# Down projections of a SwiGLU block by seven products of halves, with part of the sums on GpSimd

## The chip, the cores and the metric

The kernel runs on one core of one Trainium2 chip. A core has TensorE (PE, matrix products, with its weight loads shown apart as PEld), VectorE (DVE), ScalarE (ACT), GpSimd (POOL), SyncE (SP, which here only issues DMAs) and 16 DMA engines. Each engine works through its own instructions in order; semaphores order them against each other. SBUF is the working memory of 128 partitions, PSUM takes the results of PE. The metric is the device time of one execution in microseconds; the kernel before is given as the median of three runs.

## The reference

Two layers of a hybrid decoder on 512 tokens with 16 learned tokens ahead of them (528 columns here), model width 1024, all in float32. Each layer does an attention and retention part, and then the part that is changed:

```
hn = rmsnorm(h, ffn_norm_g)
ff = silu(hn @ w_gate) * (hn @ w_up)     # width 2816 = 22 blocks of 128
h  = h + ff @ w_down                     # back to 1024 = 8 blocks of 128
```

A last RMSNorm follows, and the 16 tokens are dropped.

## The kernel before

**Layout.** Activations lie transposed: features on the partitions, tokens on the columns. `h` is eight tiles of 128 x 528. Layer 0 works on all 528 columns in two halves of 264; in layer 1 the 16 learned tokens are no longer needed after attention, so its feed-forward part works on 512 columns (halves of 256). `w` is the width of a half.

**Precision.** Every product is made of three matmuls in a reduced format: each float32 operand is split into a high part (a cast on ACT) and a low part (a difference on DVE, in the attention stages often on POOL), and high x high, high x low and low x high are added in PSUM. So each weight block and each activation costs a split ahead of its use.

**The feed-forward loop** (`ffn`, from L794) goes over the 22 blocks of the inner width ("f blocks") in six rounds, `ROUNDS`: 0-2, 3-6, 7-10, 11-14, 15-18, 19-21. The gate and up projections of blocks 0 to 2 are dense (`dense_steps`, L217). From block 3 on a class `Unit` does gate and up of one f block together, by seven products instead of eight: the two weight matrices make up the rows of a 2 x 2 block matrix, the two halves of the model width its columns, and the two column halves of the activations the other matrix. Sums of weight blocks (`Sw`, tile `s`) and of activation blocks (`t_form`, made once per layer by `x_forms`) enter the products. A unit's weights are four conversions, the jobs `w1` to `w4`; its products are `head` (numbers 1 and 2), `middle` (6, 5, 7) and `tail` (4, 3), each of 12 matmuls (`product`, L872, matmul at L881). They accumulate into one bank from `psum_a` (x, a pool of 4 banks) and the two banks of one tile from `psum` (z and y, a pool of 2 tiles). Between products, `keep` has ACT copy the bank x into the tile `e` (L947); `done` adds z and y, applies the SiLU, multiplies, and splits the activation into `ah` and `al`, of which eight pairs of tiles exist (`act_tile`).

**Down projections** of a round are done during the next round, as fills between the products of its units: each unit takes one pair of output blocks (2p and 2p+1; four pairs in a round). `down_job` loads and splits the weights of the pair, and `down` multiplies densely: for each of the two outputs, each f block of the round, and three part products. In layer 0 there is one matmul per column half, in layer 1 one of all 512 columns (L1016). The result is copied by ACT into a tile `S` (L1023, L1025) and added into `h` by an accumulating DMA issued by POOL (L1026); in the last rounds DVE adds it. What is left when a round has only three units is done after them. The down projections of round 5 end the stage.

**Weights.** All raw weights come by DMAs issued on SP. A unit loads `w_gate`, `w_up` and half of `w_up` again into `Sw`; POOL issues two accumulating DMAs on top of these (L908, L909), so that some sums are made by the DMA. Three further sums are made by DVE (L917, L928 and the negated split L919).

**Order.** The list `steps` is the written order of PE's work. At the first matmul of a product, `need(j)` asks for the conversion of job j and of the two jobs behind it, loads included. Converted weights lie in two rings, chosen by the parity of the job's number, of two buffers each for the high and for the low part: four jobs in all. A conversion can begin when the job four before it has had its last matmul. Raw weights have three buffers (`raw`), two (`fraw`) and two (`Sw`). A scheduler of the framework puts the instructions of each engine into a fixed order ahead of the run; instructions under `high_priority` go ahead of others that are ready.

## Time and profile before

| | |
|---|---|
| median of three runs | 1272.64 us (1271.05 to 1273.75) |
| the profiled execution | 1271.96 us |
| its span, first to last instruction | 1270.1 us |
| clock granted to PE | 0.999 of full speed |

The span is what the engines' records cover; the profiled execution's own time is 1.9 us more, which lies around them. The feed-forward stages are about 300 to 616 us (layer 0) and 940 to 1240 us (layer 1). In the rows that follow, a group has its line in the kernel, its engine and operation, the tiles written and read, the shape, the count, the busy time in us, the mean of one in ns, and the engine's idle time before it with what ended it. A timeline row has start and duration in us.

### The profile page before, as it was taken

The page shows a single profiled execution, that of the slowest core. Times are in us where ns is not written, and L with a number is a line of the kernel's source. Part 1 is how long each engine was busy: PE and PEld are TensorE (multiplying, and loading weights), DVE is VectorE, ACT ScalarE, POOL GpSimd, SP SyncE. Part 2 cuts the span into 40 slices and gives each one's busy share as a digit, 9 for nine tenths or more (in the row PEclk, how much of TensorE's full clock was granted, in tenths as well). Part 3 has the DMA queues.
Part 4 walks back from the last instruction along what each step waited for, and adds up shares of the span by engine and source line. Part 5 has one row for each costly group of instructions (what it writes and reads, how often), then busy time and mean ns, then how long its engine had stood idle before and what let it go on. Part 6 is the DMA issues. An engine that isn't in the chain of part 4 may idle for free.

```text
span 1270.1 us, 24076 instructions
## 1 busy us (share of the span) xinstructions
PE 1255.0 (99%) x9271; PEld 1196.9 (94%) x9271; DVE 914.1 (72%) x1689; ACT 720.6 (57%) x1326; POOL 386.2 (30%) x662
## 2 busy tenths in 40 slices
PE   9999999999999999999999999999999999999997
PEld 8999999999999999999999989998789999999996
DVE  8877756779766666666786877477896666666766
ACT  7666545676555555554456665557765555555544
POOL 3355546421122222220025545554202222222100
PEclk9999999999999999999999999999999999999999
DMA  6322222225687777774323222222358887787721
GB/s 218 94 72 86 88 84 77 66 68 164 173 189 184 184 184 184 182 182 120 100 77 118 68 97 79 84 83 67 126 144 196 185 196 184 184 189 184 171 78 67
DMA packets 71315, 167.53 MB, mean 132 GB/s; under 512 B 8208, under 2 KB 15120, under 8 KB 71200
## 3 DMA queue, kind: packets, MB, share of 16 engines
q1 hardware_dynamic: 50576, 128.70, 31.7%
q0 software_dynamic: 20160, 36.97, 17.9%
q8 instruction: 73, 1.20, 0.4%
q14 instruction: 42, 0.34, 0.1%
q10 hardware_dynamic: 464, 0.32, 0.1%
HBM read 146.79 MB, written 2.13 MB: 117 GB/s over the span
## 4 chain that ended last, share of the span: by engine, by line
PE 92%; DVE 3%; DMA 2%; ACT 2%; issue 0%; DVEq 0%
PE psd L217 29%; PE psa L881 19%; PE psd L1016 14%; PE psd L881 13%; PE psa L217 5%; PE psa L1016 4%; PE psa L418 2%; PE psa L573 2%; PE psa L507 2%; PE psa L730 1%; PE psa L700 1%; DMA raw<-w_in 0%; DMA dec<-decay 0%; ACT whi L191 0%; PE psa L290 0%
## 5 line engine op out<-in xcount | busy, mean ns | idle before, releaser
L194 POOL TENSOR_TENSOR wlo<-raw,whi 128x128 fp32r<-128x128 f32 x504 | 259.1, 548 | 287.9 <-ACT whi L191 287.8
L217 PE MATMUL psd<-xh,whi 128*128 128x264 f32 (+1 forms) x792 | 195.8, 315 | 0.4 <-ACT whi L191 0.4
L217 PE MATMUL psd<-xh,wlo 128*128 128x264 f32 (+1 forms) x792 | 186.7, 303 | 0.0
L217 PE MATMUL psd<-xl,whi 128*128 128x264 f32 (+1 forms) x792 | 186.2, 302 | 0.4 <-DVE xl L320 0.4
L217 PEld LDWEIGHTS psd<-xh,whi 128*128 128x128 f32 x792 | 128.3, 189 | 5.4 <-ACT whi L191 1.1
L217 PEld LDWEIGHTS psd<-xh,wlo 128*128 128x128 f32 x792 | 127.0, 188 | 6.3 <-DVE wlo L194 0.4
L217 PEld LDWEIGHTS psd<-xl,whi 128*128 128x128 f32 x792 | 127.6, 189 | 4.7 <-DVE xl L320 0.8
L191 ACT CAST whi<-raw 128x512 fp32r<-128x512 f32 (+1 forms) x168 | 98.4, 613 | 49.6 <-PE psd L217 37.4
L908 POOL DMA_DIRECT2D Sw<-w_up x38 | 34.2, 899 | 230.5 <-DMA Sw<-w_up 146.4
L909 POOL DMA_DIRECT2D fraw<-w_gate x38 | 33.3, 875 | 210.5 <-DMA fraw<-w_up 65.9
L870 DVE TENSOR_TENSOR fwlo<-raw,fwhi 128x1024 fp32r<-128x1024 f32 (+2 forms) x62 | 64.0, 1033 | 38.1 <-ACT fwhi L869 38.0
L870 DVE TENSOR_TENSOR wlo<-raw,whi 128x1024 fp32r<-128x1024 f32 (+2 forms) x62 | 62.9, 1015 | 36.7 <-ACT whi L869 36.5
L869 ACT CAST whi<-raw 128x1024 fp32r<-128x1024 f32 (+2 forms) x62 | 54.9, 885 | 46.2 <-PE psd L881 37.0
L869 ACT CAST fwhi<-raw 128x1024 fp32r<-128x1024 f32 (+2 forms) x62 | 55.6, 897 | 42.8 <-PE psd L881 36.7
L917 DVE TENSOR_TENSOR Sw<-Sw,raw 128x512 f32<-128x512 f32 x38 | 26.3, 692 | 72.4 <-DMA raw<-w_gate 71.4
L1026 POOL DMA_DIRECT2D h<-S x64 | 59.9, 936 | 50.1 <-ACT S L1023 26.8
L881 PE MATMUL psa<-th,whi 128*128 128x264 f32 (+1 forms) x232 | 65.5, 283 | 0.0
L881 PE MATMUL psa<-th,wlo 128*128 128x264 f32 (+1 forms) x232 | 65.4, 282 | 0.0
L881 PE MATMUL psa<-tl,whi 128*128 128x264 f32 (+1 forms) x232 | 65.3, 282 | 0.0
L881 PE MATMUL psa<-th,fwhi 128*128 128x264 f32 (+1 forms) x224 | 63.5, 283 | 0.3 <-ACT e L947 0.3
L881 PE MATMUL psa<-tl,fwhi 128*128 128x264 f32 (+1 forms) x224 | 63.3, 283 | 0.0
L881 PE MATMUL psa<-th,fwlo 128*128 128x264 f32 (+1 forms) x224 | 63.2, 282 | 0.0
(344 smaller groups left out, 4027.3 us busy)
## 6 DMA issues: line engine op xcount, KB each, us to landing
raw<-w_in SPq DMA_DIRECT2D x54, 512.0 KB, 3.5
raw<-w_gate SPq DMA_DIRECT2D x44, 512.0 KB, 6.4
fraw<-w_up SPq DMA_DIRECT2D x38, 512.0 KB, 5.6
raw<-w_down SPq DMA_DIRECT2D x64, 256.0 KB, 2.9
Sw<-w_up SPq DMA_DIRECT2D x38, 256.0 KB, 2.6
fraw<-w_gate POOLq DMA_DIRECT2D x38, 256.0 KB, 4.3
Sw<-w_up POOLq DMA_DIRECT2D x38, 256.0 KB, 6.0
h<-S POOLq DMA_DIRECT2D x32, 264.0 KB, 5.5
```

The lines of the kernel that those rows point to most:

```text
L191: pin(nc.scalar.copy(hi, job["raw"][:, c0:c1]), pinned)
L194: pin(sub(lo[:, i:i + step], job["raw"][:, c0 + i:c0 + i + step], hi[:, i:i + step].bitcast(F32)), pinned)
L217: nc.tensor.matmul(ps[1][b][:, 0:c1 - c0], w[:, wk, :], x[:, c0:c1], start=(k == 0 and i == 0), stop=(k == n - 1 and i == 2))
L418: nc.tensor.transpose(ps[:, 128 * j:128 * j + 128], src[:, o:o + 128], idt)
L869: nc.scalar.copy(hi, src)
L870: nc.vector.tensor_sub(lo, src, hi.bitcast(F32))
L881: nc.tensor.matmul(bank()[:, 0:b.shape[-1]], a[:, o + k, :], b, start=(fresh and k == 0 and i == 0), stop=(k == n - 1 and i == 2), skip_gr ...
L908: nc.gpsimd.dma_start(s[:, HB:NK], w_up[l, self.f][:, 0:HB], accum_op=ALU.add)
L909: nc.gpsimd.dma_start(self.t["b"][:, 0:HB], w_gate[l, self.f][:, 0:HB], accum_op=ALU.add)
L917: nc.vector.tensor_add(s[:, 0:HB], s[:, HB:NK], a[:, 0:HB])
L1016: nc.tensor.matmul(v[:, 0:c1 - c0], a[:, s * n + k, :], b[:, c0:c1], start=(k == 0 and i == 0), stop=(k == n - 1 and i == 2))
L1026: nc.gpsimd.dma_start(two(h[m]), c, accum_op=ALU.add)
```

## The change

The down projections of the four rounds of four f blocks (1 to 4) no longer multiply densely. A new class `Down` takes the place of `down_job` and `down` for them: the two outputs of a pair are the rows of a 2 x 2 block matrix, the two halves of a round's four f blocks its columns, and the column halves of the activations the other matrix. Its seven products use 2 x 3 matmuls each. Parts of it:

- **Activations.** f blocks 3 to 18 no longer leave a tile pair `ah`, `al` each. When the second block of a pair of neighbours is done, seven forms of half width (blocks and their differences) are split and stored in `slots`, in two new tiles of seven forms and one of three, whose remaining four lie in halves of the state tiles `xh`, `xl` that are no longer read. POOL makes the first difference of a pair, DVE the other three. Rounds 0 and 5 keep their old tiles, which now lie in the first of the new ones. The f blocks of `w_down` are ordered on the host so that the halves lie together.
- **Weights of a Down.** POOL makes two sums and four differences of 128 x 128; one difference of 256 columns is DVE's. Fourteen blocks are split instead of eight, by two jobs.
- **Far units.** Units from f block 7 on have their sum at L917 made by POOL, in four instructions. For all units the sum of L928 goes into `s` instead of `a`, and is made at the second job instead of the fourth. Units and Downs marked `far` ask three jobs ahead instead of two.
- **Order.** From round 2 on, the products of a unit and of its Down alternate by lists written out by hand. Products 4 and 3 of a round's first Down go into the next unit (`hang`). The fourth Down of round 4 follows the units of round 5 by itself and its result is added by DVE.

```diff
         def act_tile(f):
-            return fft(f"ah{f % 8}"), fft(f"al{f % 8}")
+            t = buf(0).rearrange("p i s c -> p (i s c)")
+            i = f if f < PLAIN else f - ROUNDS[-1][0]
+            return [t[:, (2 * i + j) * T:(2 * i + j + 1) * T] for j in range(2)]
+
+        def slot(q, s, j):
+            i = (1, 2, 0)[q % 3]
+            if i < 2 or s < 3:
+                return buf(i)[:, j, s]
+            return st["x"][s - 3][j][:, HC[1][0]:HC[1][1]]
...
         def need(j):
-            for i in range(j, min(j + 3, len(jobs))):
+            for i in range(j, min(j + (4 if jobs[j].get("far") else 3), len(jobs))):
...
                     nc.gpsimd.dma_start(self.t["b"][:, 0:HB], w_gate[l, self.f][:, 0:HB], accum_op=ALU.add)
+                    if self.far:
+                        for i in range(HB):
+                            nc.gpsimd.tensor_add(s[:, i], s[:, HB + i], self.t["a"][:, i])
...
             def make2(self, hi, lo):
                 a, s = self.t["a"], self.t["s"]
-                nc.vector.tensor_add(s[:, 0:HB], s[:, HB:NK], a[:, 0:HB])
+                if not self.far:
+                    nc.vector.tensor_add(s[:, 0:HB], s[:, HB:NK], a[:, 0:HB])
                 nc.scalar.activation(hi, s, AF.Copy, scale=-1.0)
                 nc.vector.scalar_tensor_tensor(lo, s, -1.0, hi.bitcast(F32), ALU.mult, ALU.subtract)
+                nc.vector.tensor_add(s[:, 0:HB], a[:, HB:NK], s[:, 0:HB])
...
-                fh, fl = act_tile(self.f)
-                split(fh[:, c], fl[:, c], u[:, c])
-                acts[self.f] = (fh, fl)
...
+                q, second = divmod(self.f - PLAIN, 2)
+                if not second:
+                    us[q] = u2, two(tt("tq"))
+                    nc.gpsimd.tensor_sub(us[q][1][:, 0], u2[:, 1], u2[:, 0])
+                    return
+                u0, ta = us.pop(q)
+                tb = two(tt("tq"))
+                parts = [(0, 1, u0[:, 0:1]), (1, 2, u2), (3, 2, ta), (5, 2, tb)]
+                for i, (s, n, src) in enumerate(parts):
+                    if i == 2:
+                        nc.vector.tensor_sub(tb[:, 0], u2[:, 1], ta[:, 0])
+                        nc.vector.tensor_sub(tb[:, 1], u2[:, 1], u0[:, 1])
+                        nc.vector.tensor_sub(ta[:, 1], u2[:, 0], tb[:, 0])
+                    ph, pl = slots(q, s, n, 0), slots(q, s, n, 1)
+                    m = n // len(ph)
+                    for j in range(len(ph)):
+                        split(ph[j], pl[j], src[:, j * m:(j + 1) * m])
...
+        class Down:
...
+            def load(self):
...
+                r = self.t["r"] = wp.tile([128, NK, 128], F32, name="raw", tag="raw", bufs=3)
+                for s in range(2):
+                    nc.sync.dma_start(r[:, s * HB:s * HB + HB], w_down[l, 2 * self.m + s, :, self.f0:self.f1])
+                sd = self.t["s"] = tt(("nwt", "sqh")[self.m % 2])[:, 0:512].rearrange("p (k c) -> p k c", k=HB)
+                for k in range(2):
+                    nc.gpsimd.tensor_add(sd[:, 2 + k], r[:, 4 + k], r[:, 6 + k])
+                for k in range(2):
+                    nc.gpsimd.tensor_sub(sd[:, k], sd[:, 2 + k], r[:, k])
+                for k in range(2):
+                    nc.gpsimd.tensor_sub(r[:, 4 + k], r[:, k], r[:, 4 + k])
+
+            def make_a(self, hi, lo):
+                splits(hi[:, 0:HB], lo[:, 0:HB], self.t["r"][:, 0:HB])
+                splits(hi[:, HB:NK], lo[:, HB:NK], self.t["s"])
+
+            def make_b(self, hi, lo):
+                r = self.t["r"]
+                nc.vector.tensor_sub(r[:, 2:4], r[:, 2:4], self.t["s"][:, 0:2])
+                splits(hi, lo, r[:, 2:NK])
...
+            def keep(self, i):
+                def go():
+                    if i == 0:
+                        self.t["e"] = fft("S", F32, (128, 4, w), 2)
+                    e = self.t["e"][:, i]
+                    with tc.high_priority():
+                        nc.scalar.copy(e, self.t["x"][:, 0:w])
+                        if i == 3:
+                            nc.vector.tensor_add(e, self.t["y"][:, 0:w], e)
+                    if i == 2:
+                        self.add(1)
+                return go
...
+            def done(self):
+                e = self.t["e"][:, 0:2]
+                with tc.high_priority():
+                    nc.vector.tensor_add(e, self.t["zy"][:, :, 0:w], e)
+                self.add(0)
...
+                job, o, s, b, fresh, final, then = {
+                    1: (0, 0, 0, x, True, False, self.keep(0)), 2: (0, 2, 1, z, True, True, None),
+                    6: (0, 4, 5, x, False, False, self.keep(1)), 5: (0, 6, 3, y, True, False, None),
+                    7: (1, 2, 6, x, False, False, self.keep(3)), 4: (1, 4, 4, x, False, True, self.keep(2)),
+                    3: (1, 0, 2, y, False, True, self.done)}[i]
...
-                u = Unit(f)
+                u = Unit(f, r > 1)
+                if r > 1 and fills:
+                    p = fills.pop(0)[0]
+                    if p == 0:
...
+                        order = ((u, 1), (u, 2), (u, 6), (u, 5), (u, 7), (d, 1), (d, 2), (u, 4), (d, 6), (d, 5), (u, 3), (d, 7))
+                    else:
...
+                        order = [(u, 1)] + hang + [(u, 2), (d, 1), (u, 6), (d, 2), (u, 5), (d, 6), (u, 7), (d, 5), (d, 7),
+                                                   (u, 4), (d, 4), (d, 3), (u, 3)]
+                    hang = [(d, 4), (d, 3)] if p == 0 else []
+                    for o, i in order:
+                        steps += o.p(i)
+                    continue
...
             for p, g0, g1 in fills:
+                if r > 1:
+                    d = Down(p, r - 1, False)
+                    d.second()
+                    for i in (1, 2, 6, 5, 7, 4, 3):
+                        steps += d.p(i)
+                    continue
```

More of the change, by code (lines that the diff above doesn't have):

```diff
@@ L800, in ffn, with buf, slots @@
         sgs, acts = {}, {}
-        held = []
+        held, bufs, us = [], [], {}
         def two(t):
             return t[:, t0:T].rearrange("p (a b) -> p a b", a=2)
+        def buf(i):
+            if not bufs:
+                bufs[:] = [fft(f"ab{j}", shape=(128, 2, 7 if j < 2 else 3, w)) for j in range(3)]
+            return bufs[i]
         def act_tile(f):
-            return fft(f"ah{f % 8}"), fft(f"al{f % 8}")
+            t = buf(0).rearrange("p i s c -> p (i s c)")
[6 more added lines that the diff above has]
+            return st["x"][s - 3][j][:, HC[1][0]:HC[1][1]]
+        def slots(q, s, n, j):
+            i = (1, 2, 0)[q % 3]
+            return [buf(i)[:, j, s:s + n]] if i < 2 or s < 3 else [slot(q, s + k, j).unsqueeze(1) for k in range(n)]
         def g_done(f):
@@ L888, in ffn, with __init__ @@
         class Unit:
[L889 removed]
+            def __init__(self, f, far=False):
                 self.f = f
+                self.far = far
                 self.t = {}
[L892 removed]
+                self.w1 = add_job(load=self.load, make=self.make1, n=NK, far=far)
             def rest(self):
[L895 to L896 removed]
+                self.w2 = add_job(load=self.load, make=self.make2, n=NK, far=self.far)
+                self.w3 = add_job(load=self.load, make=self.make3, n=NK, far=self.far)
             def last(self):
[L899 removed]
+                self.w4 = add_job(load=self.load, make=self.make4, n=HB, far=self.far)
             def load(self):
@@ L1037, in ffn @@
         fills = []
+        hang = []
         for r, (f0, f1) in enumerate(ROUNDS):
@@ L1386 @@
     order = [0, 4, 1, 5, 2, 6, 3, 7]
+    forder = [f0 + i for f0, f1 in ROUNDS for i in ((0, 2, 1, 3) if f1 - f0 == 4 else range(f1 - f0))]
     wo = a["w_out"].reshape(DEPTH, 8, 128, D)[:, order].reshape(DEPTH, 2, 4, 128, 4, 2, 128).transpose(0, 1, 4, 3, 5, 2, 6).reshape(DEPTH, 2, 4, 128, 8, 128)
```

64 lines of the change are left out of this document (55 added, 9 removed).

## The prediction, made before the result was known

> **What bounds the kernel now.** I first read the page's shares of the engines, then how both feed-forward stages (about 300 to 616 us and 940 to 1240 us) look in a window of each, columns as on the page (PE, PEld, DVE, ACT, POOL busy with counts, granted clock, DMA share, GB/s).
>
> ```profile
> PE 1255.0 (99%) x9271; PEld 1196.9 (94%) x9271; DVE 914.1 (72%) x1689; ACT 720.6 (57%) x1326; POOL 386.2 (30%) x662
> 400.00:450.00 50.00, 50.00 (x414) 50.00 (x414) 33.21 (x46) 25.67 (x42) 11.26 (x13) 1.00 0.77 181
> 1000.00:1050.00 50.00, 49.69 (x342) 45.96 (x342) 34.68 (x47) 25.91 (x39) 10.48 (x12) 1.00 0.81 188
> ```
>
> PE never rests and its clock is full, so matmuls taken away shorten the run unless something else becomes late. DVE (66 to 69% here) is the nearest to that. The 99% does not say what a matmul costs; matmuls overlap, so I take the step from one start to the next in the timeline of PE.
>
> ```profile
> 429.80 0.29 PE L881 MATMUL psa<-xh,fwhi 128*128 128x264 f32 x1
> ...
> 437.10 0.29 PE L1016 MATMUL psa<-ah,whi 128*128 128x264 f32 x1
> ...
> 1000.54 0.40 PE L1016 MATMUL psd<-ah,whi 128*128 128x512 f32 x1
> ...
> 1002.39 0.39 PE L1016 MATMUL psd<-ah,wlo 128*128 128x512 f32 x1
> 1002.62 0.28 PE L881 MATMUL psa<-xh,whi 128*128 128x256 f32 x1
> ...
> 1005.35 0.28 PE L881 MATMUL psd<-xh,wlo 128*128 128x256 f32 x1
> ```
>
> Between the first two rows lie 60 matmuls of 264 columns: 7.30/60 = 0.1217 us each. Eight steps of 512 columns take 1.85 us: 0.231 each. Twenty-three steps of 256 columns take 2.73 us: 0.1187 each. Two matmuls of 256 cost only 0.006 us more than one of 512.
>
> **The products.** A dense down pair is 2 outputs x 4 f blocks x 3 products of high and low parts. Layer 0 does each on two column halves (48 matmuls of 264), layer 1 on all 512 columns at once (24). Seven products of halves are 7 x 2 x 3 = 42 matmuls in both layers, of 264 or 256 columns. Rounds 1 to 4 have 16 pairs per layer.
> Layer 0: 16 x 6 x 0.1217 = 11.7 us saved. Layer 1: 16 x (24 x 0.231 - 42 x 0.1187) = 16 x (5.54 - 4.99) = 8.9 us. Together 20.6 us of PE.
> A unit with its pair falls from 132 x 0.1217 = 16.06 to 126 x 0.1217 = 15.33 us in layer 0, and from 84 x 0.1187 + 24 x 0.231 = 15.51 to 14.96 us in layer 1.
> [...]
>
> **What DVE must do for it.** One unit of DVE in layer 0:
>
> ```profile
> 430.84 1.23 DVE L870 TENSOR_TENSOR fwlo<-fraw,fwhi 128x1024 fp32r<-128x1024 f32 x1 [0.60 <-ACT fwhi L869]
> 431.98 0.70 DVE L962 SCALAR_TENSOR_TENSOR tq<-sg,R 128x528 f32<-128x528 f32 x1
> 432.72 0.43 DVE L964 TENSOR_TENSOR tq<-psa,tq 128x264 f32<-128x264 f32 x1
> 433.07 0.42 DVE L965 TENSOR_TENSOR tq<-e,tq 128x264 f32<-128x264 f32 x1
> 433.52 0.69 DVE L870 TENSOR_TENSOR fwlo<-raw,fwhi 128x512 fp32r<-128x512 f32 x1
> 434.19 0.71 DVE L143 TENSOR_TENSOR al<-tq,ah 128x528 fp32r<-128x528 f32 x1
> 436.85 1.22 DVE L870 TENSOR_TENSOR wlo<-raw,whi 128x1024 fp32r<-128x1024 f32 x1 [1.94 <-ACT whi L869]
> 437.99 0.42 DVE L950 TENSOR_TENSOR e<-psd,e 128x264 f32<-128x264 f32 x1
> 438.33 0.68 DVE L928 TENSOR_TENSOR raw<-raw,Sw 128x512 f32<-128x512 f32 x1
> 440.14 0.69 DVE L917 TENSOR_TENSOR Sw<-Sw,raw 128x512 f32<-128x512 f32 x1 [1.13 <-DMA raw<-w_gate]
> 442.71 1.23 DVE L919 SCALAR_TENSOR_TENSOR fwlo<-Sw,fwhi 128x1024 fp32r<-128x1024 f32 x1 [1.87 <-ACT fwhi L918]
> 443.85 0.70 DVE L957 TENSOR_TENSOR sg<-psd,e 128x528 f32<-128x528 f32 x1
> 444.47 1.22 DVE L870 TENSOR_TENSOR fwlo<-raw,fwhi 128x1024 fp32r<-128x1024 f32 x1
> 445.60 0.70 DVE L959 SCALAR_TENSOR_TENSOR sg<-sg,R 128x528 f32<-128x528 f32 x1
> ...
> L870 DVE TENSOR_TENSOR wlo<-raw,whi 128x768 fp32r<-128x768 f32 x3 | 2.9, 953 | 1.6 <-ACT whi L869 1.6
> ```
>
> These 14 sum to 11.0 us; one starts about 0.08 us before its neighbour ends (437.99 against 436.85 + 1.22), which leaves 9.9 us of 16.06.
> Removed in a unit: the split of the pair's weights (1.22), the split of the activation (0.71), the sum at L917, which goes to POOL (0.69): 2.6 us. The sum at L928 only moves earlier.
> Added by a Down: two splits of 512 (0.69 each), a difference of 256 columns (about 0.42, the rows of 264), a split of 768 (0.95), an add of 264 out of PSUM (0.42) and one of 528 (0.70): 3.9 us.
> Added per pair of f blocks: three differences of 264 (0.42 each), splits of 264 (0.42) and of 3 x 528 (0.71 each): 3.8 us, all at the end of the pair's second unit, so 1.9 a unit.
> After: 11.0 - 2.6 + 3.9 + 1.9 = 14.2 us in some 20.5 instructions; less 20.5 x 0.08 it is 12.6 of 15.33 us, 82%. A pair's first unit needs 10.7, its second 14.5. This lies behind PE as long as weights are converted ahead; the second unit has under 1 us to spare, and what it lacks must come out of the first.
> ACT gains six 128-column weight blocks, 1.5 times 528 columns of activations and two shorter copies for each of its two longer ones. Sized at DVE's durations for the same splits that is about 2 us on 25.67/50 x 16.06 = 8.2: 10.2 of 15.33 us, two thirds, hidden.
>
> **What POOL does for it, and to DVE.** A far unit brings four sums of 128 columns, a Down six, a pair one of 264, about 10.5 a unit. No such sum stands in the feed-forward stages now. The nearest rows are POOL's weight differences of the attention stages, and DVE instructions with two SBUF operands beside them (duration min/median/max, ns):
>
> ```profile
> L194 POOL TENSOR_TENSOR wlo<-raw,whi x504: 445/461/2075, 21.9 to 896.4; 128x128 fp32r<-128x128 f32 x168
> L143 DVE TENSOR_TENSOR rql<-tq,rqh x8: 693/708/1026, 51.6 to 858.0; 128x528 fp32r<-128x528 f32 x4, 128x512 fp32r<-128x512 f32 x4
> L619 DVE TENSOR_TENSOR tq<-tq,xsw x16: 683/810/1016, 50.0 to 864.8; 128x528 f32<-128x528 f32 x12, 128x512 f32<-128x512 f32 x4
> L194 POOL TENSOR_TENSOR wlo<-raw,whi 128x128 fp32r<-128x128 f32 x504 | 259.1, 548 | 287.9 <-ACT whi L191 287.8
> ```
>
> A sum takes 0.46 us by itself, 0.55 in the mean, up to 2.1; the DVE instructions beside them grow by up to 0.33 us. [...] Bounds of the cost to DVE per unit: 0, and 10.5 x 0.33 = 3.5 us if every sum hits one. About two thirds of DVE's time in the new unit is instructions with two SBUF operands, so I take two thirds of the upper end: 2.3 us. DVE then needs 14.9 of 15.33 us: no longer free cover, but not yet the bound.
> [...]
>
> POOL in one unit now, and what its sums stand behind:
>
> ```profile
> 431.12 0.87 POOL L908 DMA_DIRECT2D Sw<-w_up  x1 [5.24 <-DMA Sw<-w_up]
> 432.13 0.86 POOL L1026 DMA_DIRECT2D h<-S  x1
> 438.00 0.86 POOL L909 DMA_DIRECT2D fraw<-w_gate  x1 [5.01 <-DMA fraw<-w_up]
> 441.04 0.86 POOL L1026 DMA_DIRECT2D h<-S  x1 [2.17 <-ACT S L1023]
> ...
> Sw<-w_up POOLq DMA_DIRECT2D x38, 256.0 KB, 6.0
> ```
>
> Four issues take 3.5 us. The far sums read what the accumulating DMA at L908 brings, 6.0 us after its issue; with the issue at L909 in between, some 5.1 us of waiting. Behind them on POOL stand the Down's sums, both accumulations into h and the next unit's accumulating loads; ACT's casts of the summed weights wait for POOL, and PSUM copies queue behind those casts. With sums at their mean: 3.5 + 5.1 + 10 x 0.55 + 0.6 = 14.7 us, inside 15.33. Bounds: at 0.46 it is 13.8, and with one more 0.70 us DVE instruction ahead of each, 20.8. I take the mean, the row of the most instances: hidden. The bytes stay as they are; 77 to 81% of DMA becomes about 85%, and I charge nothing.
>
> **Where PE stalls anew.** The PSUM bank x is copied by ACT between two products.
>
> ```profile
> 437.30 0.38 ACT L947 COPY e<-psa 128x264 f32<-128x264 f32 x1 [0.48 <-PE psa L881]
> ...
> 1005.95 0.39 PE L881 MATMUL psa<-th,fwhi 128*128 128x256 f32 x1 [0.31 <-ACT e L947]
> ```
>
> The last matmul ahead of this copy started at 436.98 (just before the row at 437.10), the copy ended at 437.68: 0.7 us; with 12 matmuls (1.46 us) between the two products PE now waits once in a while, 0.31 us here. In the new orders at least 12 matmuls stand there, so nothing is added. Only the fourth Down of round 4, which runs by itself at the end of the loop, has no product between its sixth and seventh use of x: 0.7 us per layer, 1.4 together (0 if DVE and ACT were ahead, 3 if every copy there stalls).
>
> The start of a round is the other place. The first Down's product 6 reads the last sums of the pair that has just ended. Up to now the chain from the add at 443.85 to the split of the activation (434.19 + 0.71, one period of 16.06 later: 450.96) takes 7.1 us. The differences and further splits add 1.3 + 1.8 less six overlaps of 0.08: 9.7 us. PE reaches that product after six products of 12 and two of 6 matmuls: 6 x 1.46 + 2 x 0.73 = 10.2 us. The cover of 0.5 us is less than the 2.3 us that POOL may cost DVE in a unit. Three round starts a layer (the one after round 1 has a dense pair more ahead of it) cost 0 to 2 us each; I take 1: 6 us. For DVE at 97% in 24 units I charge 0.1 us a unit, 2.4 us (0 to 0.6 each).
>
> **Sum.** Against the profiled execution (1271.96 us, of which 1.9 around the span): 20.6 - 1.4 - 6 - 2.4 = 10.8 us less: 1261.2. The median of three shown is 0.7 above that execution: 1262 us.
>
> **Rivals.**
> - The cover holds: round starts and the heavy units cost nothing, as in layer 0 now, where 414 matmuls stand in each 50 us. 1271.96 - 20.6 + 1.4 + 0.7 = 1253. For it: two thirds is a guess, and 10.7 us in first units gives time back. Against it: 14.5 us in second units.
> - DVE becomes the bound: every POOL sum hits a DVE instruction, 12.6 + 3.5 = 16.1 us a unit in layer 0 (now 16.06) and about 15.9 in layer 1 (now 15.51): 12 x 0.4 = 4.8 lost, and about 3.9 kept in the units of round 5, which keep the old activation split. 1273, no change. [...] Against: DVE's PSUM adds take one SBUF operand, and POOL can go beside them.
> - POOL becomes the bound, and the kernel is slower: sums at 0.73 (0.46 and four tenths of a 0.69 us DVE instruction ahead of each) make 3.5 + 5.1 + 7.3 + 0.7 = 16.6 us. Over 24 units 12 x 0.5 + 12 x 1.1 = 19 us: 1291. It decides from 0.70 a sum, where 16.06 is passed. For it: an in-order queue with a 6.0 us landing in its middle, and the mean of 0.55 comes from stages where DVE had fewer such instructions. Against: what stands in the wait can be put elsewhere, and weights are made three jobs ahead.
> - DVE is held for the whole 0.46 us each time: 12.6 + 4.8 = 17.4 us, 12 x 1.3 + 12 x 1.7 = 36 lost: 1309. The longest growth seen, 0.33, speaks against it. [...]
>
> **Chances.** Forecast 0.41, cover holds 0.17, DVE bound 0.16, POOL bound 0.23, whole hold 0.03. What a measurement here can tell from no change is 0.2%, 2.5 us: faster (below 1270) 0.58, the same 0.16, slower 0.26. The range runs from 1251 (nothing lost) to 1285, which leaves out most of the last two cases. The forecast's own range is 1256 to 1269.
>
> **What would show it.** PE: 96 fewer matmuls in layer 0 and 288 more in layer 1, at steps of 0.12. DVE in windows within rounds 2 to 4 at 85 to 97%, POOL near 60% busy; splits there growing by 0.3 us beside POOL sums. PE waits of some 1 us at the first Down of rounds 3, 4 and 5, released by DVE splits of the pair's slots. The forecast is wrong if PE stays full there (1253), or if PE waits in every unit: for DVE with DVE never idle (1273), or with ACT or DVE waiting for POOL's sums (1291).

## The result, and the profile after

The changed kernel takes 1317.66 us (median of 4 runs, 1314.17 to 1319.85), the kernel before 1272.22 us beside it: a ratio of 1.0354, with a 95% interval of 1.0328 to 1.038. I had forecast 1262 in a range of 1251 to 1285. The profiled execution takes 1318.31 us, its span 1316.5 us (46.4 more than before), with a mean granted clock of 0.983.

The changed kernel's shares of the engines:

```profile
PE 1259.2 (96%) x9463; PEld 1209.6 (92%) x9463; DVE 1025.4 (78%) x1896; ACT 775.0 (59%) x1502; POOL 616.8 (47%) x1002
```

There are 192 more matmuls, as worked out (96 fewer in layer 0, 288 more in layer 1), and 57.3 us in which PE has nothing to do (1316.5 less 1259.2), 42.2 more than before. Windows of it (PE, PEld, DVE, ACT, POOL busy, clock, DMA share, GB/s), the first and third around the start of round 2 in layers 0 and 1, the second right behind it:

```profile
350.00:400.00 50.00, 41.73 (x306) 41.30 (x305) 29.47 (x43) 22.31 (x37) 19.30 (x28) 0.90 0.64 142
400.00:450.00 50.00, 49.53 (x405) 49.11 (x404) 46.12 (x69) 30.79 (x56) 31.09 (x42) 1.00 0.74 176
1000.00:1050.00 50.00, 43.77 (x296) 41.35 (x296) 36.68 (x55) 24.56 (x44) 22.40 (x32) 0.90 0.67 156
```

In the steady stretch PE is nearly full, DVE at 92% and POOL at 62%, close to what I had worked out. Most of the loss sits in a few places, and there DVE and POOL are *less* busy (29.47 and 19.30 of 50 us). No engine is overloaded there; something is late. What PE waited for (total, times, longest):

```profile
PE psa L898 <- ACT S L1087: 17.0, 9, 3.4
PE psa L898 <- ACT e L968: 11.0, 6, 4.5
PE psd L898 <- DVE sg L978: 8.4, 3, 4.1
PE psd L898 <- DVE S L1089: 4.4, 9, 0.6
```

All four are PSUM banks that were not read in time: by the copies of the Downs (L1087) and of the units (L968) on ACT, and by the adds out of PSUM (L978, L1089) on DVE. With three short waits for splits (0.2 to 0.6 us) these are 42.1 us; before, PE's waits of these kinds were 0.3 us. The largest gaps, in the timeline of PE:

```profile
359.25 0.59 PE L898 MATMUL psd<-xh,whi 128*128 128x264 f32 x1 [3.80 <-DVE sg L978]
385.57 0.59 PE L898 MATMUL psa<-th,fwhi 128*128 128x264 f32 x1 [4.47 <-ACT e L968]
475.40 0.51 PE L898 MATMUL psa<-ab,fwhi 128*128 128x264 f32 x2 [1.34 <-ACT S L1087]
477.00 0.51 PE L898 MATMUL psd<-ab,fwhi 128*128 128x264 f32 x2 [0.61 <-DVE S L1089]
...
1001.68 0.58 PE L898 MATMUL psd<-xh,whi 128*128 128x256 f32 x1 [4.15 <-DVE sg L978]
1026.69 0.38 PE L898 MATMUL psa<-th,fwhi 128*128 128x256 f32 x1 [4.19 <-ACT e L968]
1117.11 0.79 PE L898 MATMUL psa<-ab,fwhi 128*128 128x256 f32 x2 [3.37 <-ACT S L1087]
```

Both layers lose their time at the same points: in round 1 (359, 1002), in the first pair of round 2 (386, 1027), and at the starts of rounds. Behind such gaps PE runs at a granted clock of 0.50 for a while (a window laid over the stretch behind the fourth row):

```profile
477.70:481.11 3.41, 3.41 (x18) 3.41 (x17) 3.40 (x6) 1.54 (x2) 0.65 (x2) 0.50 0.90 193
```

In the timeline of this stretch ten steps from one matmul's start to the next take 2.20 us (477.93 to 480.13): 0.22 us each instead of 0.121, at a clock of 0.50. The drop at 477 came behind gaps of only 1.34 and 0.61 us (the rows at 475 and 477).

The sum: in the feed-forward stages the clock is at 0.50 in eight such stretches of 3.4 or 6.8 us, 37.5 us in all. PE waits anyway in 3.9 of them, so at a clock of 0.50 I estimate the cost at (37.5 - 3.9)/2 = 17 us. The products save the 20.6 us worked out. 42 + 17 - 21 = 38 of the 46.4 us. The rest was not traced; steps too short to be listed as waits are a likely part of it, since the window from 490 to 540 us has no listed wait and holds 409 matmuls, where before the change 414 stood.

**Two places, read back to their cause.** First the gap at 385.57. POOL's queue ahead of it in the changed kernel:

```profile
369.65 0.87 POOL L927 DMA_DIRECT2D fraw<-w_gate  x1 [6.92 <-DMA Sw<-w_up]
370.19 1.23 POOL L926 DMA_DIRECT2D Sw<-w_up  x1
376.30 3.58 POOL L930 TENSOR_TENSOR Sw<-Sw,raw 128x128 f32<-128x128 f32 x4 [4.88 <-DMA Sw<-w_up]
379.82 1.78 POOL L1158 DMA_DIRECT2D h<-S  x2
380.97 1.52 POOL L1055 TENSOR_TENSOR nwt<-raw 128x128 f32<-128x128 f32 x2
382.16 1.13 POOL L1057 TENSOR_TENSOR nwt<-nwt,raw 128x128 f32<-128x128 f32 x2
382.99 1.12 POOL L1059 TENSOR_TENSOR raw<-raw 128x128 f32<-128x128 f32 x2
383.81 0.99 POOL L995 TENSOR_TENSOR tq<-tq 128x264 f32<-128x264 f32 x1
```

The last row is the first difference of a pair's activations. It needs nothing from the weights, but stands behind two loads, the far sums that wait for them and six sums of a Down. ACT in the same kernel:

```profile
384.83 0.41 ACT L142 CAST xh<-tq 128x264 fp32r<-128x264 f32 x1 [4.77 <-POOL tq L995]
385.15 0.37 ACT L968 COPY e<-psa 128x264 f32<-128x264 f32 x1
```

ACT waited 4.77 us with the cast of that difference; the PSUM copy `e` was queued behind it, and PE behind that copy. The sum's amount of work is 0.99 us; its place cost 4.5 us of PE.

Second, the gap at 359.25 in round 1, whose units are not far and use no POOL sum. SP and DVE in the changed kernel, and what SP waited for between 330 and 362 us:

```profile
339.99 0.81 SPq L1128 DMA_DIRECT2D raw<-w_down  x2
...
343.89 0.68 DVE L887 TENSOR_TENSOR fwlo<-Sw,fwhi 128x512 fp32r<-128x512 f32 x1
344.60 0.33 SPq L925 DMA_DIRECT2D Sw<-w_up  x1
...
356.75 0.69 DVE L939 TENSOR_TENSOR Sw<-Sw,raw 128x512 f32<-128x512 f32 x1 [8.92 <-issue]
358.50 0.70 DVE L978 TENSOR_TENSOR sg<-psd,e 128x528 f32<-128x528 f32 x1
```

```profile
SPq L1128 <- DVE Sw L942: 27.0, 2, 14.9
```

Of the kernel before, the same steps:

```profile
336.99 0.33 SPq L907 DMA_DIRECT2D Sw<-w_up  x1
338.48 0.80 SPq L996 DMA_DIRECT2D raw<-w_down  x2
...
348.57 0.69 DVE L917 TENSOR_TENSOR Sw<-Sw,raw 128x512 f32<-128x512 f32 x1 [1.45 <-DMA raw<-w_gate]
```

L942 is the sum that went from `a` into `s`. `s` is now held until the split of job four has read it (343.89), and the next load into it starts right behind (344.60; before 336.99). SP's order also changed: `w_down` is asked for first, and waits 14.9 us for a raw buffer. POOL issues the accumulating load on top of it only at 351.23; with the median landing of 5.5 us that ends at 356.7, where L939 starts (the profile itself names no releaser for this wait). So the sum at L939 runs 8 us later, and the PSUM add L978, queued behind it on DVE, frees PE's bank late.

### The profile page after: what moved, and what is told of

The parts are those of the page before. It is cut to its first block, busy times and chain, and to the rows that moved or that the text cites. A ratio compares the mean times of both kernels' runs of the same rounds, so it can differ in the third digit from the quotient of the medians.

```text
span 1316.5 us, 25342 instructions
## 1 busy us (share of the span) xinstructions
PE 1259.2 (96%) x9463; PEld 1209.6 (92%) x9463; DVE 1025.4 (78%) x1896; ACT 775.0 (59%) x1502; POOL 616.8 (47%) x1002
## 5 line engine op out<-in xcount | busy, mean ns | idle before, releaser
L217 PE MATMUL psd<-xh,whi 128*128 128x264 f32 (+1 forms) x792 | 195.9, 315 | 0.4 <-ACT whi L191 0.4
L930 POOL TENSOR_TENSOR Sw<-Sw,raw 128x128 f32<-128x128 f32 x120 | 87.8, 775 | 125.2 <-DMA Sw<-w_up 108.2
L887 DVE TENSOR_TENSOR wlo<-raw,whi 128x1024 fp32r<-128x1024 f32 (+2 forms) x66 | 76.7, 1163 | 21.3 <-ACT whi L886 21.1
L898 PE MATMUL psa<-th,fwhi 128*128 128x264 f32 (+1 forms) x256 | 75.0, 293 | 8.9 <-ACT e L968 8.9
L898 PE MATMUL psa<-tl,fwhi 128*128 128x264 f32 (+1 forms) x256 | 74.5, 291 | 0.0
L968 ACT COPY e<-psa 128x264 f32<-128x264 f32 (+1 forms) x114 | 42.7, 375 | 44.2 <-PE psa L898 44.1
L898 PE MATMUL psa<-ab,fwhi 128*128 128x264 f32 (+3 forms) x292 | 58.5, 290 | 9.2 <-ACT S L1087 9.0
L898 PE MATMUL psd<-xh,whi 128*128 128x264 f32 (+1 forms) x186 | 55.5, 298 | 8.0 <-DVE sg L978 8.0
L527 ACT ACTIVATE probs<-probs,nmax 128x144 f32<-128x144 f32 (+1 forms) x64 | 36.9, 576 | 44.3 <-DVE nmax L514 31.4
L1087 ACT COPY S<-psa 128x264 f32<-128x264 f32 (+1 forms) x128 | 47.2, 369 | 24.5 <-PE psa L898 24.0
L142 ACT CAST ab<-tq 128x528 fp32r<-128x528 f32 (+1 forms) x64 | 36.4, 574 | 41.2 <-DVE tq L986 23.2
```

The source lines that it names most:

```text
L142: pin(nc.scalar.copy(hi, src), pinned)
L217: nc.tensor.matmul(ps[1][b][:, 0:c1 - c0], w[:, wk, :], x[:, c0:c1], start=(k == 0 and i == 0), stop=(k == n - 1 and i == 2))
L527: nc.scalar.activation(pr, pr, AF.Exp, bias=nmax[0:nq], scale=-1.0, accum_out=rsum)
L887: nc.vector.tensor_sub(lo, src, hi.bitcast(F32))
L898: nc.tensor.matmul(bank()[:, 0:b.shape[-1]], a[:, o + k, :], b, start=(fresh and k == 0 and i == 0), stop=(k == n - 1 and i == 2), skip_gr ...
L930: nc.gpsimd.tensor_add(s[:, i], s[:, HB + i], self.t["a"][:, i])
```

## Experiments

The theory after this reading: **place**, not amount. POOL's and DVE's sums hold nothing up by the work they bring, but by the loads that they wait for with other engines' work queued behind. The rivals: **amount** (POOL or DVE has too much to do), and **contention** (POOL's sums slow DVE).

### One part at a time

`first_on_dve`: the first difference of a pair goes to DVE.

```diff
-                    nc.gpsimd.tensor_sub(us[q][1][:, 0], u2[:, 1], u2[:, 0])
+                    nc.vector.tensor_sub(us[q][1][:, 0], u2[:, 1], u2[:, 0])
```

> The first difference of a pair of f blocks (L995 of the changed kernel) is made by DVE instead of POOL; nothing else is changed. Theory 'POOL's queue': this difference stands on POOL behind the far sums, which wait up to 8.0 us for an accumulating DMA; ACT and behind it PE wait for it at four places (PE gaps of 4.5, 2.9, 4.2 and 2.7 us, 14 us together, and half clock behind three of them, 3.4 us each, which costs 5 us). Without it on POOL these go: about 19 us less than the 1317.7 us of the changed kernel, 1299 us. Rival 'DVE is the bound': DVE gets 16 more instructions of 0.42 us and its lateness only moves: within 5 us of 1317.7.

Measured 1294.28 us, 1.0173 [1.0156, 1.019]: eight instructions a layer, 23 us. DVE got more to do and the kernel faster, which speaks against amount on DVE.

`far_on_dve`: the far sums go back to DVE.

```diff
-                    if self.far:
-                        for i in range(HB):
-                            nc.gpsimd.tensor_add(s[:, i], s[:, HB + i], self.t["a"][:, i])
...
-                if not self.far:
-                    nc.vector.tensor_add(s[:, 0:HB], s[:, HB:NK], a[:, 0:HB])
+                nc.vector.tensor_add(s[:, 0:HB], s[:, HB:NK], a[:, 0:HB])
```

> The sum of a far unit (L930 of the changed kernel, four instructions on POOL) goes back to DVE as one instruction of 0.69 us; the first differences and the Downs' sums stay on POOL. Theory 'POOL's queue': the wait of the far sums for the DMA is what makes both the first differences and the Downs' sums late. Both kinds of PE gaps go (14 + 11 us, and half clock of about 12 us): 1281 us. Rival 'the number of sums on POOL': POOL is late because it has too much to do; then four of ten sums less gain at most a third of that, 1305 us. Rival 'DVE is the bound': 0.69 us a unit more on DVE, no gain.

Measured 1313.12 us, 1.0322 [1.0285, 1.036]; I had expected 1281. Its timeline shows why (DVE, then PE):

```profile
375.74 0.69 DVE L935 TENSOR_TENSOR Sw<-Sw,raw 128x512 f32<-128x512 f32 x1 [6.39 <-DMA Sw<-w_up]
377.48 0.70 DVE L974 TENSOR_TENSOR sg<-psd,e 128x528 f32<-128x528 f32 x1
378.23 0.39 PE L898 MATMUL psd<-xh,fwhi 128*128 128x264 f32 x1 [2.28 <-DVE sg L974]
```

POOL no longer waits for the load, DVE does, and the PSUM add is behind it. The wait moved from one queue to another.

`near_sum_in_a`: in round 1's units alone (four a layer) the last sum goes into `a` at job four again.

```diff
-                nc.vector.tensor_add(s[:, 0:HB], a[:, HB:NK], s[:, 0:HB])
+                if not (not self.far):
+                    nc.vector.tensor_add(s[:, 0:HB], a[:, HB:NK], s[:, 0:HB])
...
+                if not self.far:
+                    a, s = self.t["a"], self.t["s"]
+                    nc.vector.tensor_add(a[:, HB:NK], a[:, HB:NK], s[:, 0:HB])
+                    splits(hi, lo, a[:, HB:NK])
+                    return
```

> For the units of round 1 alone the sum for the fourth job is made as in the kernel before: in the raw tile and at the fourth job, so that Sw is free again once that sum is made. Theory: in the changed kernel Sw is held until the split of the fourth job, its next load starts 7 us later, the accumulating DMA lands late and DVE waits 8.9 us at L939 with the PSUM add of the unit before queued behind it; PE gaps of 3.8 and 0.9 us in layer 0, 4.1, 0.9 and 0.5 in layer 1, and half clock of 6.8 us behind the two long ones: about 17 us less, 1301 us. Rival: the load waits for something else (the order of the loads on SP); no change, 1318 us.

Measured 1289.22 us, 1.013 [1.0115, 1.0146]: 28 us, the largest of the three. No engine has less to do by this edit; a sum of the same size only stands elsewhere. The load is back in its time (SP and DVE of this kernel):

```profile
336.56 0.33 SPq L925 DMA_DIRECT2D Sw<-w_up  x1
348.23 0.69 DVE L939 TENSOR_TENSOR Sw<-Sw,raw 128x512 f32<-128x512 f32 x1 [1.57 <-DMA raw<-w_gate]
```

The gaps of round 1 are gone, and those behind them at 386 and 1027 shrink too, though L995 is still on POOL: the longest wait for `e` falls from 4.5 to 1.6 us. What is late in round 1 had been making round 2 late.

### Parts together

The same edits combined. "near" is near_sum_in_a's edit; "Downs' sums on DVE" is

```diff
-                for k in range(2):
-                    nc.gpsimd.tensor_add(sd[:, 2 + k], r[:, 4 + k], r[:, 6 + k])
...
+                nc.vector.tensor_add(sd[:, 2:4], r[:, 4:6], r[:, 6:8])
+                nc.vector.tensor_sub(sd[:, 0:2], sd[:, 2:4], r[:, 0:2])
...
+                nc.vector.tensor_sub(r[:, 4:6], r[:, 0:2], r[:, 4:6])
```

`far_dve_near`: far sums on DVE, and near.

> Both edits: far sums on DVE, and the units of round 1 make their last sum as in the kernel before. If the two causes are independent the gains add: 1317.7 - 37 - 17 = 1264 us, which is below the kernel before. If DVE is the bound, not below 1290.

`first_dve_near`: first difference on DVE, and near.

> The two edits that helped most, together: the first difference of a pair on DVE (alone 1294.3 us) and the last sum of the units of round 1 made as in the kernel before (alone 1289.2 us, from 1317.7). If they are independent the gains add, 1266 us. If part of the late first differences came from the late loads of round 1, less is left for it: of the PE gaps with the second edit 1.6, 1.5 and 2.8 us stand behind first differences, some 8 us with the half clock, which gives 1281 us.

`down_first_near`: the latter, and the Downs' sums on DVE.

> As first_dve_near, and the Downs' sums of weights are made by DVE too (three instructions of 256 columns for six of POOL); only the far sums stay on POOL. Theory 'POOL's queue': the gaps of 1.3 us behind a Down's PSUM copy, and of 0.6 us behind its add, stand behind Down sums that are late on POOL and hold ACT; they go, some 10 us less than first_dve_near. Rival 'DVE is the bound': DVE has 1.1 us more a unit, and the run is not faster than first_dve_near.

`all_dve_near`: the latter, and the far sums on DVE: no sum is left on POOL.

> No sum at all on POOL: first differences, Downs' sums and far sums on DVE, with the last sums of round 1 as before. DVE's work is some 14.6 of 15.33 us a unit in layer 0 and nothing contends with it. [...] Rival 'DVE is the bound' (it must wait for DMAs in its own order, and has no room to catch up): 1275 us or more.

| kernel | us | ratio to before [95%] |
|---|---|---|
| far_dve_near | 1286.89 | 1.0127 [1.0088, 1.0166] |
| first_dve_near | 1280.38 | 1.0059 [1.0038, 1.0079] |
| down_first_near | 1273.46 | 1.0006 [0.9995, 1.0016] |
| all_dve_near | 1270.93 | 0.999 [0.9979, 1.0002] |

From first_dve_near on, each step that takes sums off POOL makes the kernel faster, until the loss is gone (the last step by 2.5 us, with intervals that overlap). These steps alone do not separate place from contention, for both shrink with each sum that leaves POOL. The parts do not add: first difference 23 us and near 28 us alone, 37 together; near alone had already shrunk the gaps at 386 and 1027, which stand behind a first difference. With all sums on DVE a window of layer 0 is

```profile
450.00:500.00 50.00, 49.43 (x404) 48.98 (x403) 46.94 (x85) 30.89 (x58) 10.49 (x12) 1.00 0.77 182
```

DVE at 94%, PE at 99%: DVE can carry all of it, and still is not the bound. But the gain I expected (1255 to 1260) did not come. In layer 1 of this kernel ACT's rows show what is left:

```profile
1040.47 0.62 ACT L142 CAST ab<-tq 128x512 fp32r<-128x512 f32 x1 [1.22 <-DVE tq L1005]
...
1041.93 0.37 ACT L970 COPY e<-psa 128x256 f32<-128x256 f32 x1
```

The same pattern a size smaller: ACT waits 1.22 us for a difference of the activations, with a PSUM copy queued behind.

`all_dve_in_a` and `down_first_in_a`: as all_dve_near and down_first_near, with the last sum in `a` for all units.

> As all_dve_near (1270.9 us), but all units, not those of round 1 alone, make their last sum in the raw tile at the fourth job, so that Sw is free before the split of the fourth job. Theory 'late loads': the waits for the accumulating DMA that hold DVE's and POOL's queues in the far units get shorter too; 1262 to 1267 us. Rival: in the far units it is the raw tile that is short, since the Downs' weights need it too; then holding it until the fourth job makes the loads later, 1275 us or more.

> As down_first_near (1273.5 us), with the last sum in the raw tile for all units; far sums on POOL. The same two theories: 1266 us if Sw is what is late, 1277 or more if it is the raw tile. Against all_dve_in_a it shows what the far sums on POOL cost or save where Sw is free earlier.

Measured 1276.74 us, 1.0034 [1.0017, 1.005], and 1299.09 us, 1.02 [1.0183, 1.0217]. What frees `s` sooner in round 1 holds `a`, a raw buffer, longer, and in the far units raw buffers are what is short: of the changed kernel,

```profile
SPq L1052 <- DVE Sw L942: 195.1, 30, 14.6
```

is SP waiting for L942's release of one before it can load a Down's weights. The slower run shows it itself: between 385 and 1210 us of down_first_in_a, POOL's far sums wait 64.1 us for `w_gate` (into `a`), and DVE waits 41.3 us for `w_down`, against 21.3 in down_first_near.

### Amount, or place

`no_sums_near`: all_dve_near with the weights' sums of the far units and Downs left out.

```diff
-                nc.vector.tensor_add(s[:, 0:HB], s[:, HB:NK], a[:, 0:HB])
+                if not self.far:
+                    nc.vector.tensor_add(s[:, 0:HB], s[:, HB:NK], a[:, 0:HB])
+                src = a if self.far else s
...
-                splits(hi[:, HB:NK], lo[:, HB:NK], self.t["s"])
+                splits(hi[:, HB:NK], lo[:, HB:NK], self.t["r"][:, HB:NK])
```

> Leaves out the sums: the far sums and the Downs' six sums of weights are made by no engine, and the weights are split as they are; first differences on DVE, last sums of round 1 as before. It shows what the rest of the change costs (order of products, splits, PSUM copies). If sums are the whole loss: 1272.9 - 20.6 + 1.4 for the Down that runs by itself = 1254 us. If the new order of products has stalls of its own, 1262 us or more.

Measured 1295.39 us, 1.0181 [1.0161, 1.0201]: DVE has less to do, and the kernel is 24 us *slower* than all_dve_near. DVE and PE at one of its gaps:

```profile
399.64 0.69 DVE L941 TENSOR_TENSOR Sw<-raw,Sw 128x512 f32<-128x512 f32 x1 [6.41 <-DMA Sw<-w_up]
401.52 0.39 PE L898 MATMUL psa<-xh,wlo 128*128 128x264 f32 x1 [2.97 <-DVE wlo L887]
```

With the first sum gone, the last one, which now reads the late load itself, came to stand ahead of a split PE needs at once. So DVE's amount of work does not decide: less of it in a worse order cost more than all the sums.

`before_plus_pool` and `before_pool_done`: the kernel before, with ten idle sums of 128 x 128 on POOL in each unit from f block 7 on, that nobody waits for: at the load, from constants, or when the activation is done, from it.

```diff
+                    if self.f >= 7:
+                        for _ in range(10):
+                            nc.gpsimd.tensor_add(tmp.tile([128, 128], F32, name="dm", tag="dm", bufs=1), idt, msk)
```

```diff
+                if self.f >= 7:
+                    for i in range(10):
+                        nc.gpsimd.tensor_add(tmp.tile([128, 128], F32, name="dm", tag="dm", bufs=1), u[:, t0:t0 + 128], u[:, t0 + 128:t0 + 256])
```

> The kernel before, with ten sums of 128 x 128 on POOL added to each unit from f block 7 on (30 units), of two constant tiles into a scratch tile that nobody reads: POOL's work and its contention with DVE, with no result that anyone waits for. Theory 'the place in the queues': the work by itself is covered, 1273 to 1277 us, although DVE's instructions beside the sums grow by 0.3 us. Rival 'contention and POOL's time': 30 units lose about 0.7 us or more each, 1293 us or more.

> The kernel before, with ten sums of 128 x 128 on POOL per unit from f block 7 on, of parts of the unit's activation into a scratch tile that nobody reads, issued when the activation is done: POOL's time and its contention with DVE in the feed-forward stages, but no wait for a DMA of their own and no reader. Theory 'the place in the queues': within 4 us of the kernel before, although DVE's instructions beside them grow. Rival 'contention and POOL's time': 15 us or more lost.

The first measured 1398.1 us, 1.0978 [1.0962, 1.0995], and does not answer the question it was for. Its sums had no input to wait for, and went to where they delayed something else (all instances of the line, then PE's wait):

```profile
L912 POOL TENSOR_TENSOR dm<-idt,msk x300: 447/452/969, 15.9 to 217.5; 128x128 f32<-128x128 f32 x150
```

```profile
PE psd L217 <- POOL wlo L194: 78.6, 10, 17.1
```

All 300 ran in the first attention stage, ahead of the weight differences that PE needs there: some 136 us of POOL's time (300 x 0.452). It says nothing of the feed-forward stages.

The second measured 1273.2 us, 1.0006 [0.9997, 1.0015]: no cost. A window of it, the ten sums of one unit in the timeline of POOL, and the group of DVE's activation splits between 400 and 616 us, here and then in the kernel before:

```profile
400.00:450.00 50.00, 50.00 (x413) 50.00 (x413) 35.24 (x44) 26.13 (x43) 31.52 (x44) 1.00 0.76 185
```

```profile
434.78 7.35 POOL L968 TENSOR_TENSOR dm<-tq 128x128 f32<-128x128 f32 x10
```

```profile
L143 DVE TENSOR_TENSOR al<-tq,ah 128x528 fp32r<-128x528 f32 x14 | 13.7, 977 | 0.0
```

```profile
L143 DVE TENSOR_TENSOR al<-tq,ah 128x528 fp32r<-128x528 f32 x14 | 9.9, 709 | 0.2
```

Contention is real: a split grows from 709 to 977 ns, a sum to 0.735 us (7.35/10). POOL is as busy as in the changed kernel (31.5 of 50 us), and PE stays full. The growth, 0.27 us, is some six tenths of 0.46 us, the median of POOL's 128 x 128 differences in the kernel before (461 ns). At DVE's 70% (35.24 of 50 us) it costs nothing here (ratio 1.0006). So POOL's amount of work by itself does not hold PE up; contention beside a fuller DVE is the next runs' matter.

### What is left

`ad_late_pool`: all_dve_near, with one of the Downs' differences, wanted last, on POOL again.

```diff
+                for k in range(2):
+                    nc.gpsimd.tensor_sub(r[:, 4 + k], r[:, k], r[:, 4 + k])
...
-                nc.vector.tensor_sub(r[:, 4:6], r[:, 0:2], r[:, 4:6])
```

`ad_subs_first`: all_dve_near, with the three remaining differences of the activations written ahead of the splits.

```diff
+                nc.vector.tensor_sub(tb[:, 0], u2[:, 1], ta[:, 0])
+                nc.vector.tensor_sub(tb[:, 1], u2[:, 1], u0[:, 1])
+                nc.vector.tensor_sub(ta[:, 1], u2[:, 0], tb[:, 0])
                 for i, (s, n, src) in enumerate(parts):
-                    if i == 2:
-                        nc.vector.tensor_sub(tb[:, 0], u2[:, 1], ta[:, 0])
...
```

`pool_subs_first`: ad_subs_first, with the far and the Downs' sums on POOL.

> As all_dve_near (1270.9 us), but the difference of a Down's weights that only its second job reads is made by POOL (two instructions). If DVE's load is what holds PE there, some 3 us faster; if places in the queues, no faster, and slower where ACT or DVE now wait for POOL.

> As all_dve_near, but the three differences of a pair's activations are written ahead of all its splits, so that ACT's casts do not wait for them with PSUM copies behind. If that wait is what holds PE (gaps of 0.6 to 1.2 us behind ACT's copy e in three or four units a layer), some 5 us faster, 1266; if not, the same.

> As ad_subs_first (1268.1 us), but the far sums and the Downs' sums of weights are on POOL as in the changed kernel; first differences on DVE, last sums of round 1 as before, the three other differences ahead of the splits. Theory 'the place in the queues': POOL's sums of weights stand behind waits for the DMA and stay late: 1275 us or more. Rival: what was wrong was the activations alone; then POOL relieves DVE of 1.8 us a unit and it is 1263 us or less.

ad_late_pool measured 1277.69 us, 1.0042 [1.0022, 1.0062], 6.8 us more than all_dve_near. A place in POOL's queue does not explain it directly: in its trace no engine waits for these POOL differences. What changes is DVE beside them. Its splits of activations between 400 and 600 us:

```profile
L143 DVE TENSOR_TENSOR ab<-tq,ab 128x528 fp32r<-128x528 f32 x15 | 11.1, 751 | 0.0
```

In all_dve_near this group takes 702 ns, and its splits of 128x1024 out of `raw` 1219 ns against 1325 here. The difference taken off DVE was 5.9 us of work in these 200 us (14 of 0.42), but DVE is busy only 2.3 us less (182.4 against 184.7). So contention, which cost nothing at 70% in before_pool_done, is the likely cause beside a DVE at over 90%; that DVE's order changed too is not ruled out.

pool_subs_first measured 1279.38 us, 1.0044 [1.003, 1.0057], 11.3 us more than ad_subs_first. Here both are in the trace: between 385 and 1210 us ACT waits 17.7 us for POOL's sums of the Downs (11 times), and the two groups of splits take 807 and 1582 ns.

ad_subs_first measured 1268.1 us, 0.9963 [0.995, 0.9977], and beats both kernels. Its windows, two in layer 0 and one in layer 1, and what PE still waits for in the feed-forward stages:

```profile
400.00:450.00 50.00, 50.00 (x413) 50.00 (x412) 45.36 (x82) 30.55 (x55) 10.49 (x12) 1.00 0.82 201
550.00:600.00 50.00, 49.85 (x410) 49.64 (x409) 47.81 (x85) 30.84 (x56) 11.30 (x13) 1.00 0.72 168
1100.00:1150.00 50.00, 48.41 (x404) 47.57 (x403) 45.75 (x82) 30.27 (x54) 11.30 (x13) 1.00 0.79 184
```

```profile
PE psd L898 <- DVE S L1088: 3.5, 5, 1.0
PE psa L898 <- ACT S L1086: 2.6, 2, 1.3
PE psa L898 <- ACT e L970: 2.0, 4, 1.0
```

In layer 0 PE is full but for the Down that runs by itself, as before the change, with 96 fewer matmuls to do. In layer 1 it still loses 0.2 to 1.0 us in each of several units; the two waits of 1.2 and 1.3 us for L1086 are that Down, one in each layer.

`asf_u3_first`: ad_subs_first, with the unit's product 3 ahead of the Down's in the written order.

```diff
-                                                   (u, 4), (d, 4), (d, 3), (u, 3)]
+                                                   (u, 4), (d, 4), (u, 3), (d, 3)]
```

> As ad_subs_first, with the unit's product 3 ahead of the Down's product 3 in the units of the second to fourth pair, so that 12 more matmuls lie between the Down's seventh product and the one that waits for its add. If the gaps of 0.5 to 1.0 us in layer 1 are that wait, they go, some 4 us less: 1264 us. Rival: the Down's last add then comes later and the next product 2 waits for its PSUM tile; 1268 us or more.

Measured 1339.94 us, 1.0523 [1.0508, 1.0537]. In this order the last pair of a round overwrites forms that the Down's product 3 has not read, so that product takes the next round's forms, which changes part of the computation, and PE waits up to 7.2 us at a round's end for the whole chain of activations. The time does not speak to what the run was for.

## Why the prediction was wrong

- **PE's saving: right.** "20.6 us of PE" from steps of 0.121, 0.119 and 0.231 us. The steps came out the same (121, 119 and 232 ns as medians), and in layer 0 of ad_subs_first most of the gain is there: the first matmul behind its feed-forward stage starts at 636.4 us instead of 645.6, 9.2 us earlier of the 11.7 worked out. The whole profiled execution is 6.6 us shorter (1265.34 against 1271.96), so layer 1 showed nothing of its 8.9; its PE still waits there.
- **"The sum at L928 only moves earlier": this step failed first.** I costed it at nothing and named no work that hides it. It also changed where the sum goes, and so when `s` and `a` come free. Undoing it in eight units gave back 28 us. Of its two effects, `s` held to job four and SP's changed order in round 1, near_sum_in_a restores both. For the load at 344.60 the trace points to `s`: SP had come to it, and waited 1.6 us more for the split of job four. No run restores one of the two alone.
- **"With sums at their mean ... I take the mean ...: hidden": the sum was nearly right and the conclusion was not.** Between 385 and 585 us of the changed kernel POOL works for 126.0 us and waits for loads for 59.2: 15.4 us for each of the 12 units, against 14.7. The sums took longer than their 0.55 us (0.775 in the mean of L930), the wait ahead of L930 was shorter (108.2 us in 26 waits, 4.2 a time, against 5.1). I had even named what stands behind the far sums: the Downs' sums, accumulations, and ACT's casts with PSUM copies behind them. I then asked only whether it all fits into a unit. first_on_dve shows what one sum in that queue is worth: 23 us. The rival "POOL becomes the bound" has the right sign and the right engine, and nearly the time of a sum (0.73, an estimate, against 0.775). With 15.4 us against the 15.33 of a unit, POOL had in fact hardly any room to catch up once it was late. But it does not give the loss: that rival has PE wait in every unit, and here 13 gaps of over 1 us make up 34 of the 42 us; near_sum_in_a leaves POOL's work as it was and gives 28 us back, while far_on_dve takes the far sums and their waits off POOL and gives 4.5.
- **Half clock behind gaps: not in the sum at all.** Some 17 us, two fifths of what the gaps themselves cost.
- **Round starts, "I take 1: 6 us": the chain was right, its size depends on the rest.** With L995 on POOL the starts cost up to 4.5 us; in ad_subs_first, layer 0 has no gap there.
- **The lone Down, "0.7 us per layer": mis-sized.** Its gap is 1.28 us in layer 0 of the changed kernel, 1.40 and another 0.5 in layer 1.
- **"DVE then needs 14.9 of 15.33 us": about right.** 92% in the changed kernel, 91 to 96% in ad_subs_first, where DVE makes all the sums. Its rival "DVE becomes the bound" is refuted by that same kernel. "Whole hold" needs 17.4 us of DVE in a unit, and DVE was not full at 92%; the mean growth in before_pool_done, 0.27 us, is less than the 0.46 it takes. The two thirds counted only instructions with two SBUF operands. In the changed kernel adds out of PSUM did not grow: L971 took 409 to 434 ns, also at 533.81 us beside the longest of POOL's sums (0.42 us), and L1105 675 to 708; `tq<-e,tq` (L986), of L971's width and with both operands in SBUF, took 408 to 681.

Open: the waits of up to 1 us in layer 1 of ad_subs_first, behind PSUM adds at L1088, where DVE has 4 us of 50 to spare; and how the 7 to 11 us that POOL's sums cost beside a DVE at over 90% divide between contention and place: ad_late_pool points to contention, and no run has the one without the other. A fourth raw buffer, the plain answer to SP's waits, was not tried.

## What to carry to other kernels

When work is moved to an engine that seems idle, don't ask only whether its time fits; write down its queue in order, mark each entry that waits for a DMA, and ask who waits for what stands behind it. A change of the tile that a result goes into is a change of when two buffers come free, and must be followed to the next load of each. Give PSUM reads a queue in which nothing ahead of them waits.

## What the runs showed of the hardware

- The granted clock fell to half for 3.4 us behind gaps of PE of only 1.34 and 0.61 us, with matmuls in between; a like pair in the same kernel (1.20 and 0.61 us, ahead of the rows at 541.66 and 543.27) brought no drop: the clock is 1.00 from 541 to 551 us. In the changed kernel half clock took an estimated 17 us beside gaps of 42.
- A sum of 128 x 128 on POOL took 0.45 us at its shortest and up to 3.5 us beside a DVE without a break (minimum, median and maximum in ns):

```profile
L930 POOL TENSOR_TENSOR Sw<-Sw,raw x120: 447/642/3513, 376.3 to 1256.0; 128x128 f32<-128x128 f32 x120
```

A median of 642 and a maximum of 3513 ns. In the 3.5 us of the longest, from 530.70 us on, DVE was busy throughout and began eight instructions; my upper bound had one 0.70 us instruction of DVE ahead of each sum.
